# A rotation of a large matrix by 90 degrees: smaller transposing pieces and one more output buffer

## The chip, the cores and the metric

The kernel runs on one core of a Trainium2 chip. The metric is the device time of that core in microseconds (us); the median of the kernel before is 1267.99 us over 3 runs (1267.86 to 1268.66). The profile's own span of a run is about 2 us shorter than its time. No run of this study was recorded in the slow state, so all comparisons are between runs recorded as fast. A few single runs were nonetheless about 10 us longer than their fellows (one of the changed kernel, two of one experiment, and one 6 us longer); medians are quoted for that reason, and no reading rests on these runs.

## The reference

```python
def setup_inputs():
    return {"x": np.random.randn(8192, 8192).astype(np.float32), "k": 1}

def reference(x, k):
    return np.rot90(x, k)
```

No arithmetic is wanted: 268.44 MB are read, 268.44 MB are written, and every element changes its place.

## The kernel before

Each load brings 128 rows of 4096 columns (2 MB) on SyncE's queue. VectorE copies the load in chunks of `CH` columns with the columns of each block of 128 reversed, which empties the load buffer. TensorE transposes the blocks into PSUM (the tiles `pt` of the kernel), ScalarE copies PSUM into an output buffer of 2 MB, and ScalarE's queue stores it.

```python
R, W, CH, F, FP = 1024, 4096, 512, 4096, 2048      # RT = 8 loads per tile
...
a_pool = ctx.enter_context(tc.tile_pool(name="a_pool", bufs=2))    # loads
r_pool = ctx.enter_context(tc.tile_pool(name="r_pool", bufs=68))   # chunks
o_pool = ctx.enter_context(tc.tile_pool(name="o_pool", bufs=2))    # outputs
...
# load: for each of the rt blocks of 128 rows
nc.sync.dma_start(out=a[:], in_=x[r0 + t*P : r0 + (t+1)*P, c0 : c0 + W])
for j in range(W // CH):
    ar = r_pool.tile([P, CH // P, P], dt, tag="ar")
    nc.vector.tensor_copy(out=ar[:],
        in_=a[:, j*CH : (j+1)*CH].rearrange("r (b m) -> r b m", m=P)[:, :, ::-1])
    chunks[t, j] = ar
...
# store: for each half group (16 transposes of 128x128)
nc.tensor.transpose(ps[:, PW-1-w, t*P : (t+1)*P],
                    chunks[t, g*P // CH][:, g % (CH // P), :], ident)
nc.scalar.copy(o[:, G-PW-h : G-h, :], ps)
# when S blocks are filled
nc.scalar.dma_start(out=dst, in_=o[:, G-done : G-done+S, :])
```

There are 128 loads and, but for the last in two halves, 128 stores of 2 MB. With chunks of 512 columns VectorE makes 8 copies per load, 1024 in all.

Of the kernel before, what the change touches and what calls it, by code (L numbers as in the profile page):

```python
# [2 lines left out]

# [5 lines left out]

P = 128  # L10




R = 1024
RT = R // P
LAST = [4, 4]
W = 4096
CH = 512
F = 4096  # L20
FP = 2048


def whole_reads(nc):






    for fn in nc.m.functions:
        for block in fn.blocks:
            for n, ins in enumerate(block.instructions):
                if not isinstance(ins, mybir.InstDMACopy):
                    continue
                src = ins.ins[0]
                ap = [list(d) for d in src.ap]
                if len(ap) == 3 and ap[2][0] == 1 and ap[1][0] == ap[2][1]:
                    ap = [ap[0], [1, 1], [1, ap[1][1] * ap[2][1]]]
                    block.instructions[n] = copy.replace(  # L40
                        ins,
                        ins=[copy.replace(src, ap=ap)],
                        ant_dge_precooked=False,
                    )


def macro_tiles(N, M):

    tiles = [(r0, RT, c0) for r0 in range(0, N, R) for c0 in range(0, M, W)]
    r0, _, c0 = tiles.pop()  # L50
    for n in LAST:
        tiles.append((r0, n, c0))
        r0 += n * P
    return tiles


@with_exitstack
def kernel(
    ctx: ExitStack,
    tc: tile.TileContext,  # L60
    x: bass.AP,
    k: bass.AP,
    out: bass.AP,
):
    nc = tc.nc
    assert k == 1, f"only k=1 supported, got {k}"
    nc.at_finalize(whole_reads)

    N, M = x.shape
    dt = x.dtype  # L70

    consts = ctx.enter_context(tc.tile_pool(name="consts", bufs=1))
    ident = consts.tile([P, P], dt)
    make_identity(nc, ident)

    a_pool = ctx.enter_context(tc.tile_pool(name="a_pool", bufs=2))
    r_pool = ctx.enter_context(tc.tile_pool(name="r_pool", bufs=68))
    o_pool = ctx.enter_context(tc.tile_pool(name="o_pool", bufs=2))
    psum_pool = ctx.enter_context(
        tc.tile_pool(name="psum", bufs=2, space=bass.MemoryType.PSUM)  # L80
    )

    loads = 0

    def load(r0, rt, c0):





        nonlocal loads
        chunks = {}
        for t in range(rt):


            if loads < RT and loads % 4 >= 2:
                a = o_pool.tile([P, W], dt, tag="o")
            else:
                a = a_pool.tile([P, W], dt, tag="a")
            loads += 1  # L100
            nc.sync.dma_start(
                out=a[:], in_=x[r0 + t * P : r0 + (t + 1) * P, c0 : c0 + W]
            )
            for j in range(W // CH):
                ar = r_pool.tile([P, CH // P, P], dt, tag="ar")
                nc.vector.tensor_copy(  # L106
                    out=ar[:],
                    in_=a[:, j * CH : (j + 1) * CH].rearrange(
                        "r (b m) -> r b m", m=P
                    )[:, :, ::-1],  # L110
                )
                chunks[t, j] = ar
        return chunks

    def store(r0, rt, c0, chunks, end):





        rows = rt * P
        PW = 1
        while 2 * PW * rows <= FP:
            PW *= 2
        G = PW
        while 2 * G * rows <= F:
            G *= 2
        for i, g0 in enumerate(range(0, W // P, G)):
            if end and i % 2 == 0:
                ot = a_pool.tile([P, F], dt, tag="a")  # L130
            else:
                ot = o_pool.tile([P, F], dt, tag="o")
            o = ot[:, : G * rows].rearrange("m (g f) -> m g f", g=G)

            S = PW if end and r0 + rows == N and g0 + G == W // P else G
            for h in range(0, G, PW):
                pt = psum_pool.tile([P, FP], mybir.dt.float32, tag="ps")
                ps = pt[:, : PW * rows].rearrange("m (g f) -> m g f", g=PW)
                for w in range(PW):
                    g = g0 + h + w  # L140
                    for t in range(rt):
                        nc.tensor.transpose(  # L142
                            ps[:, PW - 1 - w, t * P : (t + 1) * P],
                            chunks[t, g * P // CH][:, g % (CH // P), :],
                            ident,
                        )
                nc.scalar.copy(o[:, G - PW - h : G - h, :], ps)  # L147

                done = h + PW
                if done % S == 0:  # L150
                    top = M - c0 - (g0 + done) * P
                    dst = out[top : top + S * P, r0 : r0 + rows].rearrange(
                        "(g m) f -> m g f", g=S
                    )
                    nc.scalar.dma_start(  # L155
                        out=dst, in_=o[:, G - done : G - done + S, :]
                    )

    tiles = macro_tiles(N, M)
    *most, before_last, last = tiles  # L160
    for m in most:
        store(*m, load(*m), False)

    c1 = load(*before_last)
    c2 = load(*last)
    store(*before_last, c1, True)
    store(*last, c2, True)


# [1 line left out]
_INS = ['x', 'k']  # L171
_OUTS = [((8192, 8192), 'float32')]

_NUMBERS = {'k': 1}


# [26 lines left out]
```

## Time and profile before

| | before |
|---|---|
| time, median of 3 | 1267.99 us |
| span of the profiled run | 1266.0 us |
| DMA, mean over the span | 425 GB/s |
| TensorE / ScalarE / VectorE busy | 55% / 37% / 28% |
| VectorE copies | 1024 of 512 columns |

The page gives each engine's busy time, then the span in 40 slices, of which the GB/s row matters most here. The prediction below shows those lines. Two kinds of lines also belong here: the DMA queues that carry no data of the kernel, and the time from issue to landing of the stores. These are from the page of the kernel before; a queue's line gives its packets, its MB and its share of the DMA engines' time.

```profile
q8 instruction: 32, 0.52, 0.2%
q14 instruction: 17, 0.14, 0.0%
...
out_dram<-ot ACTq DMA_DIRECT2D x127, 2048.0 KB, 15.9
```

The two queues of the kind "instruction" I take to bring the engines their programs. At 0.2% and 0.0% they look like nothing, and I passed over them.

### The profile page before, as it was taken

How to read it: one execution, taken by the hardware profiler on the slowest of the kernel's cores; microseconds unless marked ns; L12 is line 12 of the kernel's file. 1: busy time of each engine (PE TensorE's matmuls, PEld its weight loads, DVE VectorE, ACT ScalarE, POOL GpSimd, SP SyncE). 2: the span in 40 equal slices, each digit the busy share in tenths (PEclk: the TensorE clock that was granted, in tenths of full speed). 3: DMA queues.
4: the chain of work that ended last, by engine and by line, in shares of the span. 5: the costliest groups of instructions: out<-in, count | busy, mean ns of one | idle time of the engine just before them, and what ended most of it. 6: DMA issues, size and time to landing. Idle time of an engine off the chain costs nothing.

```text
span 1266.0 us, 10386 instructions
## 1 busy us (share of the span) xinstructions
PE 700.4 (55%) x4096; PEld 660.8 (52%) x4096; DVE 354.9 (28%) x1024; ACT 467.3 (37%) x257; POOL 0.7 (0%) x6
## 2 busy tenths in 40 slices
PE   1456455665655555555556546565464665656573
PEld 0355455554545455554555445464464654556573
DVE  4422322232222322233222322233222332223210
ACT  0333334333433334333433334333433334333364
POOL 0000000000000000000000000000000000000000
PEclk9986777777678777787777877778777667777687
DMA  9999999999999999999999999999999999999998
GB/s 398 416 431 429 429 428 429 430 427 430 427 429 429 429 429 430 428 429 428 430 428 428 429 429 427 427 429 426 430 429 427 414 428 430 426 427 428 428 393 370
DMA packets 37057, 537.55 MB, mean 425 GB/s; under 512 B 4112, under 2 KB 4112, under 8 KB 4112
## 3 DMA queue, kind: packets, MB, share of 16 engines
q10 hardware_dynamic: 18576, 268.44, 50.0%
q1 hardware_dynamic: 18432, 268.44, 49.9%
q8 instruction: 32, 0.52, 0.2%
q14 instruction: 17, 0.14, 0.0%
HBM read 268.44 MB, written 268.44 MB: 424 GB/s over the span
## 4 chain that ended last, share of the span: by engine, by line
DMA 78%; ACT 19%; issue 1%; DVE 1%; ACTq 0%; PE 0%; DVEq 0%
DMA out_dram<-ot 74%; ACT ot L147 19%; DMA a<-in_x_dram 3%; DVE ar L106 1%; ACTq L155 0%; PE pt L142 0%; ACTq L147 0%; DVEq L106 0%
## 5 line engine op out<-in xcount | busy, mean ns | idle before, releaser
L142 PE MATMUL pt<-ident,ar 128*128 128x128 f32 x4096 | 700.4, 350 | 548.3 <-ACT ot L147 465.9
L142 PEld LDWEIGHTS pt<-ident,ar 128*128 128x128 f32 x4096 | 660.8, 187 | 587.7 <-ACT ot L147 496.4
L147 ACT COPY ot<-pt 128x2048 f32<-128x2048 f32 x256 | 466.0, 1869 | 742.6 <-DMA out_dram<-ot 729.5
L106 DVE COPY ar<-a 128x512 f32<-128x512 f32 x1024 | 354.9, 420 | 865.8 <-DMA a<-in_x_dram 811.4
L147 ACT ACT_TABLE_LOAD x1 | 1.3, 1283 | 41.1 <-DVE ar L106 41.1
masks.py:199 POOL TENSOR_SCALAR_AFFINE_SELECT ident<-ident 128x128 f32<-128x128 f32 x1 | 0.3, 294 | 0.1
masks.py:197 POOL MEMSET ident<- 128x128 f32 x1 | 0.2, 205 | 0.3 <-POOLq L184 0.3
L184 POOL MEMSET const-bfloat16-1.0<- 128x1 bf16 x1 | 0.1, 102 | 0.0
L184 POOL MEMSET const-uint8-127<- 128x1 uint8 x1 | 0.1, 102 | 0.0
L184 POOL MEMSET const-float32-0.0<- 128x1 f32 x1 | 0.1, 99 | 0.2 <-issue 0.2
L184 POOL MEMSET const-float32-1.0<- 128x1 f32 x1 | 0.1, 99 | 0.0
## 6 DMA issues: line engine op xcount, KB each, us to landing
a<-in_x_dram SPq DMA_DIRECT2D x128, 2048.0 KB, 16.8
out_dram<-ot ACTq DMA_DIRECT2D x127, 2048.0 KB, 15.9
out_dram<-ot ACTq DMA_DIRECT2D x2, 1024.0 KB, 13.7
```

The source lines that it names most:

```text
L106: nc.vector.tensor_copy(out=ar[:], in_=a[:, j * CH : (j + 1) * CH].rearrange("r (b m) -> r b m", m=P)[:, :, ::-1],)
L142: nc.tensor.transpose(ps[:, PW - 1 - w, t * P : (t + 1) * P], chunks[t, g * P // CH][:, g % (CH // P), :], ident,)
L147: nc.scalar.copy(o[:, G - PW - h : G - h, :], ps)
L184: nc = _bacc.Bacc("TRN2", target_bir_lowering=False, num_devices=1)
```

## The change

The intent: a third output buffer should let ScalarE run further ahead of the stores, so that the DMA engines do not run dry when the loads end. Its 2 MB must come from somewhere, so the pool of chunks shrinks from 68 of 512 columns (8.5 loads' worth) to 127 of 256 (just under 8 loads, which is a whole tile); smaller chunks should come free sooner and make up for it. The first outputs go out in halves, to start the stores earlier.

```diff
-CH = 512
+CH = 256
-    r_pool = ... bufs=68
-    o_pool = ... bufs=2
+    r_pool = ... bufs=127
+    o_pool = ... bufs=3
-            if loads < RT and loads % 4 >= 2:
+            if loads < RT and loads % 5 >= 2:
-            if end and i % 2 == 0:
+            if end and i % 2:
                 ot = a_pool.tile([P, F], dt, tag="a")
-            S = PW if end and r0 + rows == N and g0 + G == W // P else G
+            starts = r0 == 0 and c0 == 0 and i < 2 or end and r0 + rows < N and i == 0
+            ends = r0 + rows == N and c0 + W == M and g0 + G == W // P
+            S = PW if starts or ends else G
 ...
-    c1 = load(*before_last)
-    c2 = load(*last)
-    store(*before_last, c1, True)
-    store(*last, c2, True)
+    *_, chunks = load(*before_last)
+    outputs = store(*before_last, chunks, True)
+    rows = load(*last)
+    for _ in range(last[1] - 1):
+        next(rows)
+    next(outputs)            # first end group ahead of the last load
+    chunks = next(rows)
+    for _ in outputs: ...
+    for _ in store(*last, chunks, True): ...
```

(`load` and `store` become generators that yield after each load and each group.)

More of the change, by code (lines that the diff above doesn't have):

```diff
@@ L76 @@
     a_pool = ctx.enter_context(tc.tile_pool(name="a_pool", bufs=2))
-    r_pool = ctx.enter_context(tc.tile_pool(name="r_pool", bufs=68))
-    o_pool = ctx.enter_context(tc.tile_pool(name="o_pool", bufs=2))
+    r_pool = ctx.enter_context(tc.tile_pool(name="r_pool", bufs=127))
+    o_pool = ctx.enter_context(tc.tile_pool(name="o_pool", bufs=3))
     psum_pool = ctx.enter_context(
@@ L112, in load @@
                 chunks[t, j] = ar
-        return chunks
+            yield chunks
     def store(r0, rt, c0, chunks, end):
@@ L157, in store @@
                     )
+            yield
     tiles = macro_tiles(N, M)
@@ L161 @@
     for m in most:
-        store(*m, load(*m), False)
-    c1 = load(*before_last)
-    c2 = load(*last)
-    store(*before_last, c1, True)
-    store(*last, c2, True)
+        *_, chunks = load(*m)
+        for _ in store(*m, chunks, False):
+            pass
+    *_, chunks = load(*before_last)
[5 more added lines that the diff above has]
+    chunks = next(rows)
+    for _ in outputs:
+        pass
+    for _ in store(*last, chunks, True):
+        pass
 _INS = ['x', 'k']
```

## The prediction

> **What bounds the kernel now.** I read the page first: busy shares, slices, the chain that ended last. Then the waits by pair, and last the time windows in steps of 100, 5 and 1 us, to find where the DMA engines are not full.
>
> ```profile
> span 1266.0 us, 10386 instructions
> PE 700.4 (55%) x4096; PEld 660.8 (52%) x4096; DVE 354.9 (28%) x1024; ACT 467.3 (37%) x257; POOL 0.7 (0%) x6
> ...
> GB/s 398 416 431 429 429 428 429 430 427 430 427 429 429 429 429 430 428 429 428 430 428 428 429 429 427 427 429 426 430 429 427 414 428 430 426 427 428 428 393 370
> ...
> DMA 78%; ACT 19%; issue 1%; DVE 1%; ACTq 0%; PE 0%; DVEq 0%
> L106 DVE COPY ar<-a 128x512 f32<-128x512 f32 x1024 | 354.9, 420 | 865.8 <-DMA a<-in_x_dram 811.4
> ```
>
> No engine is busy more than 55% of the span, while the GB/s row stays at 426 to 431 in 35 of the 40 slices. The chain is DMA for 78%; the 19% of ACT in it is copying while other transfers run, so it is no cost by itself. The waits say the same from the other side:
>
> ```profile
> DVE ar L106 <- DMA a<-in_x_dram: 811.4, 121, 8.1
> ACT ot L147 <- DMA out_dram<-ot: 729.5, 118, 6.9
> ```
>
> VectorE waits for a load 121 times and ScalarE for an output buffer 118 times, out of 128 of each: both sides stand behind the same transfers. A queue that waits for its buffer costs nothing as long as the other queue, or an earlier transfer of its own, fills the engines. So the question is only where both run dry.
>
> ```profile
> 0.00:5.00 5.00, 0.00 (x0) 0.00 (x0) 0.00 (x0) 0.00 (x0) 0.70 (x6) 1.00 0.65 226
> ...
> 100.00:1100.00 1000.00, 563.81 (x3252) 534.21 (x3253) 280.11 (x809) 371.24 (x204) 0.00 (x0) 0.74 1.01 428
> ...
> 1214.00:1215.00 1.00, 1.00 (x6) 1.00 (x6) 0.00 (x0) 1.00 (x1) 0.00 (x0) 0.50 0.43 180
> 1215.00:1216.00 1.00, 1.00 (x7) 1.00 (x6) 0.00 (x0) 0.43 (x1) 0.00 (x0) 0.50 0.16 66
> 1216.00:1217.00 1.00, 1.00 (x8) 1.00 (x7) 0.00 (x0) 0.00 (x0) 0.00 (x0) 0.66 0.69 295
> ```
>
> The last two columns are the DMA share and GB/s. In the middle 1000 us the share is 1.01 and the rate 428. The hole stands at 1214 to 1217.
>
> The account: 537.55 MB in all, at the 429 GB/s of the best long stretches, take 537.55 / 0.429 = 1253.0 us. The span has 13.0 more. By windows of 5 us, each charged with (429 minus its rate) / 429 of its length: the first 5 us lose 2.4 (no byte can move before the first load starts); 45 to 65, when stores join the loads, lose 0.9 (426, 416, 374, 423); 1210 to 1225 lose 2.3 (378, 334, 374); 1225 to 1260, where only stores are left, lose 0.9 (410 to 423); the last 6 us hold only 193 GB/s over 5 us and lose 3.75 (the last bytes land and are confirmed). That is 10.3; the other 2.7 are the difference of 426 to 428 from 429 over the long middle.
>
> Why there is a hole at 1214, from the timeline:
>
> ```profile
> 1205.62 0.55 ACTq L155 DMA_DIRECT2D out_dram<-ot  x1
> 1208.10 2.77 DVE L106 COPY ar<-a 128x512 f32<-128x512 f32 x8 [7.04 <-DMA a<-in_x_dram]
> 1211.80 3.63 ACT L147 COPY ot<-pt 128x2048 f32<-128x2048 f32 x2 [6.21 <-DMA out_dram<-ot]
> ...
> 1215.46 0.55 ACTq L155 DMA_DIRECT2D out_dram<-ot  x1
> 1217.14 3.65 ACT L147 COPY ot<-pt 128x2048 f32<-128x2048 f32 x2 [1.71 <-PE pt L142]
> ```
>
> With two output buffers one store is in flight while the other buffer waits for its landing (1211.72), is filled for 3.63 us, and is issued at 1215.46. While loads share the engines a store takes 9.8 us of them and that turnaround is hidden. The last load is issued at 1201.1; when its bytes run out, the one store left finishes in half the time and nothing is queued behind it. Then at 1217.14 ScalarE waits 1.71 us for TensorE, which could not begin that group before ScalarE freed PSUM at 1213.7.
>
> [...] here a load takes 4.9 us alone (copies start at 8.10, 12.99, 17.88) and 9.8 us beside stores. [...]
>
> **The change part by part.**
> 1. *Chunks of 256.* 2048 VectorE copies for 1024. [...] Sixteen per load are 3.4 us for 2.77: +0.6 per load, 80 us of busy time in all, 28% to about 34%. None of it is on the path: VectorE sits 7.0 us idle before each load in the steady stretch. A load buffer comes back 0.6 us later, with another load already queued.
> 2. *127 chunks of 256 for 68 of 512.* A tile of 8 loads uses 128 of the small ones. The spare goes from 4 large (half a load) to minus 1 small, but chunks come free after each half group rather than each group. In the built programs VectorE's copies take the chunks in the order in which TensorE frees them, so one group of stores makes room for one load in both.
> 3. *Third output buffer.* ScalarE, and TensorE behind it, run one group further ahead of the stores. That frees one load's worth of chunks earlier, more than the half load lost in part 2. Steady rate unchanged: the DMA share is already 1.01. At the end two stores (about 10 us of engine time at 4.9 to 5.0 each) instead of one stand queued when the last load's bytes run out, against a turnaround of about 4 us (3.63 + 0.1 of issue and a start): the hole at 1210 to 1225 should close. I count 2.0 of its 2.3 us.
> 4. *First outputs in halves.* The first store goes after one copy, about 1.9 us sooner than 49.65. But loads fill the engines at 419 to 433 GB/s until 50, so it only reorders. Of the 0.9 lost at 45 to 65 I count 0.3. Three more issues at 0.55 us of ScalarE's queue are beside 6 us waits. The first group of the next-to-last piece in halves helps the same hole as part 3, not a second one.
> 5. *Five load buffers at the start for four.* Loads alone already run at about 430 GB/s with four; nothing.
> 6. *The last load's chunks allocated after the first end group.* Needed because 8 loads of chunks no longer fit; TensorE has that group early, so no wait follows.
>
> Sum: -2.0 - 0.3 = -2.3 us; 1268.0 - 2.3 = 1265.7.
>
> **Rivals.**
> *Chunks become the wait.* With no spare, VectorE waits for TensorE, a load buffer stays full, loads pause. For it: VectorE already waited 54.4 us on TensorE, 7 times, up to 12.0. Against: during those waits (55.8 to 67.8) stores kept the share at about 1, and three output buffers give TensorE more lead. If it emptied the load queue for 1 us in each of the 15 later tiles, the time would be about 1280.
> *It was hidden anyway.* The hole merely moves later, for instance to ScalarE's pace at the end (4.31 us per group against about 5.0 of DMA). Then 1268 stays. Against: ScalarE is the faster of the two, and its last copy ends 11 us before the DMA engines go quiet.
> *A larger gain.* All of 2.3 and 0.9, and 428 becoming 429 through the deeper store queue (1100 us x 1/429 = 2.6): 1262. Against: a share of 1.01 leaves nothing for a deeper queue to fill.
>
> **Range and chances.** Fixed losses (2.4 first, 3.75 last, 0.9 for stores alone) and the 1253.0 put the floor near 1260 of span, 1262 of time (the time is 2.0 above the span). Gain between 0 and 5 us, so 1262.8 to 1268.2 for 8 in 10. Two per cent is 25 us, twice all the time that is not at full rate: faster by that is nearly excluded; slower by that would need a new wait in every tile.
>
> **What would show it.** Right: the GB/s row unchanged in the middle; its last two slices up from 393 and 370; no window under 300 GB/s between 1205 and 1250; VectorE near 435 us busy and its copies near 212 ns apart; ScalarE's waits for stores still the largest of its waits. Wrong: VectorE waiting for TensorE well above 54 us together with steady windows under 425; a hole left at the end of the loads; or a first slice different from 398 by more than 10.

## The result, and the profile after

| | before | after |
|---|---|---|
| median of 6 runs | 1267.97 us | 1274.97 us |
| lowest to highest | 1267.50 to 1268.66 | 1274.66 to 1284.05 |
| ratio of fast runs | | 1.0066, 95% interval 1.0039 to 1.0093 |

The kernel became 7.0 us slower by the medians. That is within 2%, as I had expected, but outside my range and in the other direction. A ratio here is the mean time of one kernel's fast runs over that of the other's of the same rounds, so it isn't quite the ratio of the medians; the one run of 1284 us lifts it.

The page of the changed kernel answers to the lines of the prediction:

```profile
span 1272.9 us, 11534 instructions
PE 702.6 (55%) x4096; PEld 662.8 (52%) x4096; DVE 425.6 (33%) x2048; ACT 466.8 (37%) x257; POOL 0.7 (0%) x6
...
GB/s 397 423 427 428 428 428 429 428 429 429 428 429 427 429 429 430 428 429 428 429 430 428 426 424 427 427 427 423 429 424 427 425 423 423 428 426 419 424 374 328
...
q14 instruction: 26, 0.21, 0.0%
...
DMA 82%; ACT 13%; DVE 2%; PE 2%; ACTq 0%; issue 0%; SPq 0%; DVEq 0%
L106 DVE COPY ar<-a 128x256 f32<-128x256 f32 x2048 | 425.6, 287 | 796.7 <-DMA a<-in_x_dram 578.2
...
out_dram<-ot ACTq DMA_DIRECT2D x124, 2048.0 KB, 25.6
```

The bound is still DMA, with 82% of the chain. VectorE's busy time is 425.6 us. The rate starts as before, but sinks in the second half: of the slices from the 22nd on many read 423 to 426, where before had mostly 426 to 430. The last two are 374 and 328, against 393 and 370, where I had expected a rise. A store lands 25.6 us after its issue instead of 15.9, which only says that more stores are under way: with one issued every 9.8 us (median, both kernels) 2.6 on average for 1.6, an estimate from these three numbers.

The waits of the changed kernel, by pair (total us, times, longest):

```profile
ACT ot L149 <- DMA out_dram<-ot: 698.9, 113, 8.8
DVE ar L106 <- DMA a<-in_x_dram: 578.2, 94, 8.0
...
DVE ar L106 <- PE pt L144: 218.6, 34, 7.8
```

The page now puts 34 of VectorE's waits, 218.6 us, down to TensorE, that is to a free chunk (54.4 us and 7 times before). That is the line that I had named as the sign of my first rival. It is a temptation: the line has grown by 164 us, the time by 7, and it need not be the cause. In the trace the copy that ends each of the 34 waits also starts 0.09 to 0.12 us after the 16th landing of a load, so each of them was a wait for a load as well.

The windows of the changed kernel at the end of the loads and at the very end (stretch, us, busy time of five engines, granted clock, DMA share, GB/s):

```profile
1100.00:1200.00 100.00, 57.23 (x326) 54.43 (x325) 33.78 (x163) 36.35 (x20) 0.00 (x0) 0.74 1.01 424
...
1216.00:1217.00 1.00, 1.00 (x5) 1.00 (x6) 0.00 (x0) 1.00 (x1) 0.00 (x0) 0.50 0.54 229
1217.00:1218.00 1.00, 1.00 (x7) 1.00 (x6) 0.00 (x0) 0.70 (x1) 0.00 (x0) 0.50 0.27 115
1218.00:1219.00 1.00, 1.00 (x6) 1.00 (x5) 0.01 (x1) 0.00 (x0) 0.00 (x0) 0.50 0.43 180
...
1260.00:1265.00 5.00, 0.00 (x0) 0.00 (x0) 0.00 (x0) 0.00 (x0) 0.00 (x0) 0.50 0.98 408
1265.00:1270.00 5.00, 0.00 (x0) 0.00 (x0) 0.00 (x0) 0.00 (x0) 0.00 (x0) 0.50 0.22 90
...
1269.00:1270.00 1.00, 0.00 (x0) 0.00 (x0) 0.00 (x0) 0.00 (x0) 0.00 (x0) 0.50 0.06 25
```

Two things are to be seen. There is still a hole at 1216 to 1219, though another store now stands in the queue. And the end has a tail of more than 5 us in which the DMA share is 0.22, or as much as 3 to 4 engines of 16. Before, the stretch 1260 to 1265 held 193 GB/s and the next microsecond none. From 1268 to 1271 the share is 0.06 in each microsecond, which is one engine of 16. So most DMA engines finish, and a few, in the end one, do not. The GB/s row, a mean of 16 engines, can't show that.

### One level below the page: 16 landings per transfer

The trace has 16 landing events for each of the 257 transfers of before and the 260 of after, as many as the page has DMA engines; I take each to be one engine's. The next instruction starts after the 16th: in the changed kernel VectorE's first copy after each of the 128 loads starts 0.02 to 0.12 us after the 16th landing, when the first is 5.9 us past (median). So I read the time of this kernel, bound by DMA, as that of its slowest DMA engine.

I therefore took from the trace's records of landings, for each transfer in order, the time of its 16th landing, counted from the start of the span, less 4.877 us for each 2 MB landed so far (two 1 MB halves count as one). 4.877 us is the steady time of 2 MB where nothing disturbs (4.873 to 4.883 from the first to the last landing on each of the treads below that begin at 715 or later), so what remains is the time that the slowest DMA engine has lost. (These records are in the packed trace; no view of the page shows them, and they don't name the DMA engine. That it is the same one over a stretch is inferred from how its losses add up. Where the loads end the number falls by about two us (24.0 to 21.6 and 22.4 in the changed kernel), I suppose because fewer transfers are under way at once; so compare like stages.) The changed kernel between 694 and 1214 us, one number per change:

```
time of landing  lost by the slowest engine (us, from 16.3 at 694)
694 to 704       0.00
715 to 773       0.95
779 to 833       1.90
843 to 902       2.86
908 to 961       3.81
972 to 1031      4.75 to 4.86
1036 to 1090     5.78
1101 to 1155     6.74
1160 to 1214     7.68
```

It is a staircase. On a tread, 12 or 13 transfers in a row, the loss moves by a few hundredths of a microsecond, in one place by a tenth; then it jumps by about 0.95 us within one or two transfers. Set beside the 8 KB packets of the queue q14 the jumps have an owner. Eight of them start at 708, 777, 837, 906, 966, 1035, 1095 and 1155 us: one at each jump, and no jump without one. (Three others, at 797, 980 and 1114 us, leave no mark on the slowest DMA engine.) They take 309 ns. In the records a 16 KB read packet of the loads begins 0.31 us after each, as the fetch ends, and takes 1211 to 1216 ns in place of the usual 611. Together that is 0.31 + 0.60 = 0.91 us of one DMA engine. Before 694 us the changed kernel's picture is less clean: from about 260 to 655 us the slowest DMA engine is mostly another, which slips by some 0.11 us per load without such fetches, and the one with the steps follows close behind. The cleanest case is e1 below: from 150 to 1200 us its slowest DMA engine loses 15.4 us, and 16 such fetches lie there, 0.96 us each.

I take these packets for VectorE's instructions, because their number follows VectorE's: the trace has 1358 instruction records of VectorE before and 2505 after, 1147 more, and the page has 26 packets on q14 for 17, 9 more. That is one packet of 8 KB for about 127 instructions (an estimate from these two differences). VectorE doesn't stand still for it: the starts of its copies of one load are at most 0.211 us apart in the whole trace of after (median 0.202). But one DMA engine does.

| | before | after |
|---|---|---|
| 8 KB fetches followed by a read of over 1.2 us, whole span | 11 | 18 |
| of these from 150 to 1200 us | 9 | 16 |
| distance between them | about 118 us | 60 to 69 us |
| loss of the slowest DMA engine at 150 us | 8.5 | 9.3 |
| at 700 us | 12.4 | 16.3 |
| at 1200 us | 17.3 | 24.0 |
| at the last landing | 16.5 | 23.3 |

(Each loss but the last is a mean over the last four transfers before that time.) At 1200 us the difference is 6.7 and at the last landing 6.8, of the 6.9 by which the spans differ. From 150 to 1200 us the slowest engine loses 14.7 us after and 8.8 before, so 5.9 of the 6.7 arise there, evenly. Seven fetches more at 0.95 would make 6.7. It is less because before, from about 294 us on, the slowest DMA engine is another one, which slips by about 0.08 us at each load without any fetch and has besides two steps of 0.8 us, at fetches of q14 at 346 and 975 us that are not in VectorE's rhythm; the engine with VectorE's fetches ended 1.4 us ahead of it.

### The profile page after: what moved, and what is told of

Its sections match the earlier page's. It is cut to its first block, busy times and chain, and to the rows that moved or that the text cites. A ratio compares the mean times of both kernels' runs of the same rounds, so it can differ in the third digit from the quotient of the medians.

```text
span 1272.9 us, 11534 instructions
## 1 busy us (share of the span) xinstructions
PE 702.6 (55%) x4096; PEld 662.8 (52%) x4096; DVE 425.6 (33%) x2048; ACT 466.8 (37%) x257; POOL 0.7 (0%) x6
## 4 chain that ended last, share of the span: by engine, by line
DMA 82%; ACT 13%; DVE 2%; PE 2%; ACTq 0%; issue 0%; SPq 0%; DVEq 0%
DMA out_dram<-ot 71%; ACT ot L149 13%; DMA a<-in_x_dram 11%; DVE ar L106 2%; PE pt L144 2%; ACTq L157 0%; ACTq L149 0%; SPq L101 0%; DVEq L106 0%
## 5 line engine op out<-in xcount | busy, mean ns | idle before, releaser
L106 DVE COPY ar<-a 128x256 f32<-128x256 f32 x2048 | 425.6, 287 | 796.7 <-DMA a<-in_x_dram 578.2
## 6 DMA issues: line engine op xcount, KB each, us to landing
out_dram<-ot ACTq DMA_DIRECT2D x124, 2048.0 KB, 25.6
```

The source lines that it names most:

```text
L106: nc.vector.tensor_copy(out=ar[:], in_=a[:, j * CH : (j + 1) * CH].rearrange("r (b m) -> r b m", m=P)[:, :, ::-1],)
```

## The experiments

The theory after this reading is **fetch**: twice as many VectorE instructions mean twice as many fetches, each of which holds up the same one DMA engine for 0.95 us. The rivals are **depth** (the third output buffer lets the DMA engines drift apart and costs time), **chunks** (the pool with no spare makes VectorE wait for TensorE, and loads are late) and, later, **turnaround** (16 small copies return a load buffer 0.6 us later). Every run below gave a correct result and was timed against the kernel before in 5 rounds. Ratios are to before in the same rounds; the medians of before were 1267.99 in the first four runs, 1267.84 in the next four and 1268.62 in the last four (three groups on three chips).

| run | what it is | median us | ratio (95%) | loss of the slowest engine at 150 / 700 / 1200 us |
|---|---|---|---|---|
| e1 | before, chunks of 256, 136 of them | 1274.76 | 1.0052 (1.0040 to 1.0064) | 8.5 / 16.2 / 23.9 |
| e2 | after, chunks of 512 | 1267.32 | 1.0001 (0.9987 to 1.0015) | 8.7 / 12.6 / 16.4 |
| e3 | after, two output buffers | 1277.67 | 1.0098 (1.0071 to 1.0126) | 8.8 / 16.9 / 24.7 |
| e7 | after, half the chunks on GpSimd | 1270.85 | 1.0023 (1.0010 to 1.0035) | 9.6 / 13.7 / 19.4 |
| e8 | before, chunks of 1024 | 1266.85 | 0.9990 (0.9977 to 1.0002) | 8.2 / 11.3 / 15.6 |
| e9 | before, each chunk by two copies | 1273.99 | 1.0045 (1.0033 to 1.0058) | 8.2 / 16.2 / 23.0 |
| e10 | before, chunks of 128 | 1314.81 | 1.0371 (1.0357 to 1.0385) | 10.1 / 35.1 / 58.1 |
| e12 | after, first outputs whole | 1275.65 | 1.0058 (1.0046 to 1.0071) | 8.4 / 17.1 / 24.9 |

Not in this table are e4, e5 and e6, which became something else than what I meant, and e11, in which another wait took over.

### e1: the small chunks alone

```diff
-CH = 512
+CH = 256
-    r_pool ... bufs=68
+    r_pool ... bufs=136
```

> Kernel before with chunks of 256 alone (136 of them, the same memory as 68 of 512; two output buffers). Three theories for the 7.0 us lost. Fetch theory (1024 more VectorE instructions are fetched by the same DMA engines, ten more 8 KB fetches, and one DMA engine that already lags carries them): slower than before by 3 to 7 us, last landing spread over the 16 engines near 6 us instead of 2.8. Depth theory (the third output buffer lets the 16 DMA engines drift apart, 18 us between first and last of one store instead of 8 to 9, and the end pays for it): as before, within 1 us. Chunk theory (no spare chunk, VectorE waits for TensorE): as before, since there are spares here.

1274.76 us. Two output buffers, a full pool, whole first outputs, the old order at the end, and the loss is all there, in the time and in the staircase (23.9 at 1200 us). So depth, and a pool with no spare, are not needed for it. Two things did not come as expected. The spread of the last landing is 2.1 us and not near 6. And by the page VectorE waits longer for TensorE even with spare chunks; the runs e8 and e3 show why that wait is no measure of the loss:

```profile
DVE ar L106 <- PE pt L142: 190.5, 28, 11.5
DVE ar L106 <- PE pt L142: 82.8, 14, 7.4
DVE ar L106 <- PE pt L144: 83.5, 112, 2.0
```

The lines are those of e1, e8 and e3, in this order. e8 and e3 have the same 83 us of it in total, and their medians are 10.8 us apart (1266.85 and 1277.67).

### e2: everything but the small chunks

```diff
 # the changed kernel with
-CH = 256
+CH = 512
-    r_pool ... bufs=127
+    r_pool ... bufs=63
```

> Changed kernel with chunks of 512 again (63 of them, as 127 of 256 one or two short of a tile), everything else as changed: three output buffers, halves, end order. Fetch theory: back near 1268 or below, since the instruction count is that of before. Depth theory: stays near 1275, spread of one store still 15 to 18 us. Chunk theory: at or above 1275, since room comes back in whole groups only and VectorE waits longer for TensorE (above 219 us in all).

1267.32 us, where before stands at 1267.99: the loss is gone with the small chunks. The first and last landing of a transfer lie up to 13.8 us apart in this run, 9.5 in before and 18.7 in the changed kernel, so a third buffer does let the DMA engines drift further apart; but that in itself costs nothing here. This run is also the fair test of my prediction's idea, the third buffer by itself. The medians give it 0.7 us of the 2.3 that I had promised, and the ratio 1.0001 gives it none.

### e3: the third buffer taken back

```diff
 # the changed kernel with
-    o_pool ... bufs=3
+    o_pool ... bufs=2
-            if loads < RT and loads % 5 >= 2:
+            if loads < RT and loads % 4 >= 2:
```

> Changed kernel with two output buffers again (and four load buffers at the start), 127 chunks of 256 kept. Fetch theory: stays at 1271 to 1275. Depth theory: back to 1267 to 1269, spread of one store at most 9 us. Chunk theory: slower than the changed kernel, above 1276, as TensorE loses its lead and VectorE waits longer for chunks.

1277.67 us, slower than the changed kernel by 2.7 in the medians, so depth as a cost is refuted: the third buffer helps here. The fetch theory alone had given 1271 to 1275, so the size is missed. The chunk theory's number, above 1276, is met, but not its wait: by the page VectorE waits 83.5 us for TensorE, less than the 218.6 of the changed kernel. This kernel has 127 chunks where e1, also with two buffers, had 136 and took 2.9 us less, and the end is arranged differently. The landings put more than half of the 2.9 at the end: between 1232 and 1247 us, where only stores are left, e3's slowest DMA engine goes from 23.1 to about 25.0 and e1's from 22.3 to 22.6. What in the end's order does it, and the rest, stay open.

### e4, e5, e6: three tries that tested something else

To test the count of instructions or the turnaround by themselves I added idle work on VectorE to the kernel before: one `memset` of one column per chunk (e4), a copy of one column out of the load buffer per chunk (e5), and one copy of 1024 columns more per load (e6).

```diff
+    scrap = consts.tile([P, 1], dt)            # e6: [P, 1024]
 ...
 # one of these:
+                nc.vector.memset(scrap[:], 0.0)                                      # e4, per chunk
+                nc.vector.tensor_copy(out=scrap[:], in_=a[:, j*CH : j*CH + 1])       # e5, per chunk
+            nc.vector.tensor_copy(out=scrap[:], in_=a[:, :1024])                     # e6, per load
```

> Kernel before with 1024 one-column memsets on VectorE, which add instructions and no data. Fetch theory: slower than before by 3 to 7 us, with about 8 more 8 KB instruction fetches, as e1. Depth and chunk theories: as before within 1 us.

> Kernel before with a one-column VectorE copy after each of its 1024 copies (it reads the load buffer, so it cannot be moved away as the memsets were). The traces of before and changed show the slowest of the 16 DMA engines jump by about 0.95 us at each 8 KB fetch of VectorE's instructions, every 118 us before and every 60 us after. Fetch theory: the instruction count is that of the changed kernel, so the fetches come every 60 us, that engine loses 10 x 0.95 more, and the time is 1272 to 1277. Turnaround theory (VectorE gives a load buffer back 0.6 us later): the tiny copies also lengthen it by some 0.6 us, so 1272 to 1277 too; the next run tells the two apart. Third possibility, that the copies of 256 columns themselves matter: 1268.

> Kernel before with one VectorE copy of 1024 columns more for each load: about 0.61 us [...] later release of each load buffer, as in the changed kernel (3.33 for 2.77 us), with only 128 more instructions, one more fetch. Fetch theory: within 1.5 us of before. Turnaround theory: slower by about 7 us, as e1.

(The text of e5 puts the jumps of before on its slowest DMA engine; from 294 us on they are on the second slowest. e6's 0.61 us was an estimate of mine; in its trace such a copy is 0.61 us from its start, at 629.57, to the next one's, at 630.18.)

They took 1291.65, 1594.76 and 1524.90 us, and none of it says anything on fetches. The added instructions didn't stay where I had written them. In e4, the timeline (start, us, group) shows them drawn forward:

```profile
115.74 5.59 DVE L113 MEMSET scrap<- 128x1 f32 x45
```

45 of them run in a row in the first part of the kernel, where the rate falls to 287 GB/s in a slice; once they are used up (the last starts at 260.8 us), the rate is 419 to 430 in each slice until the last two. In e6 the added copy of the *next* load stands amid the copies of this one:

```profile
629.57 0.69 DVE L114 COPY scrap<-a 128x1024 f32<-128x1024 f32 x1 [14.38 <-DMA a<-in_x_dram]
```

VectorE waits 14.4 us for a load there, and the first of the eight copies behind it in its queue starts only at 630.18. By my reading four of them are of the load before, whose buffer can't be returned until then. The loads then go one at a time: SyncE waits for VectorE before 116 of them, 1238.9 us in all. In e5 it is the same, before 115 loads and for 1443.9 us. So these are kernels with a new wait, and the lesson is to look at the order of instructions, and not just at the source, before a run is spent.

### e7: the same chunks, half of VectorE's instructions

```diff
 # the changed kernel with
-                nc.vector.tensor_copy(
+                by = nc.gpsimd if j % 2 else nc.vector
+                by.tensor_copy(
```

> Changed kernel with every second chunk copied by GpSimd, so that neither engine's instruction stream has more than VectorE's had before. Fetch theory: no single DMA engine carries all the fetches, so faster than the changed kernel by 4 to 7 us (1268 to 1271), if GpSimd's fetches go through another DMA engine; as the changed kernel (1275) if they go through the same one. Turnaround theory: GpSimd's copies are slower, so the buffers come back later still, and it is slower than 1275.

1270.85 us, 4.1 less than the changed kernel. This tells fetch from turnaround, because the turnaround stays the same: from the timeline, VectorE and GpSimd work side by side and are done 3.36 us after the first copy began, against 3.33 in the changed kernel. GpSimd's copies are a little slower, as the turnaround theory had it (eight in 3.34 us for 3.11 of VectorE's eight), but a load buffer comes back only 0.03 us later.

```profile
606.17 3.11 DVE L107 COPY ar<-a 128x256 f32<-128x256 f32 x8 [6.74 <-DMA a<-in_x_dram]
606.19 3.34 POOL L107 COPY ar<-a 128x256 f32<-128x256 f32 x8 [6.51 <-DMA a<-in_x_dram]
```

The number of instructions and of q14 fetches is no lower than in the changed kernel:

```profile
q14 instruction: 28, 0.23, 0.0%
```

But the fetches in VectorE's rhythm now come about every 109 us, 11 with a read of over 1.2 us in the span for 18, and the others do not add to them on the slowest DMA engine. So it isn't the sum of fetches that counts but how many one DMA engine gets. The loss at 1200 us is 19.4, and 2.1 above before; what is left is the slipping engine, at 0.10 us per load in place of 0.08.

### e8 and e10: larger and smaller chunks in the kernel before

```diff
-CH = 512
+CH = 1024      # e8, r_pool bufs=34
+CH = 128       # e10, r_pool bufs=272
```

> Kernel before with chunks of 1024 (34 of them): half of its VectorE instructions, fetches every 200 us or more. Fetch theory: that DMA engine gains 5 x 0.95, but another DMA engine, 1.4 us behind it already in the trace of before, stays, so 0 to 1.5 us faster than before at most. Turnaround theory: 0.3 us less per load, faster by up to 3 us. If room for chunks in larger pieces matters, slower.

> Kernel before with 272 chunks of 128: 4096 VectorE copies. Fetch theory, as a dose: about 20 fetches more than e1, 20 x 0.95 = 19 us more on the DMA engine that carries them, so 1288 to 1298. If the number of instructions matters otherwise (a threshold, a phase between the DMA engines): no such proportion, 1270 to 1280.

e8 took 1266.85 us. Its page:

```profile
span 1264.3 us, 9798 instructions
...
q14 instruction: 12, 0.10, 0.0%
```

There are 12 fetches for 17, of VectorE's 5 with a read of over 1.2 us for 11. The gain is about 1 us by the medians, as expected small, because in before the slowest DMA engine is already the one that slips, not the one with the fetches. The interval of its ratio ends at 1.0002, so that it is faster isn't shown. It has the lowest median of the study all the same.

e10 took 1314.81 us. The direction is right, but it overshoots the 1288 to 1298 that I had written down. VectorE has 4096 copies and a fetch about every 40 us, and the steps are there, from 0.95 to 1.6 us each; but from 150 to 1200 us the slowest DMA engine loses 48.0 us, and the 26 fetches of that stretch at 0.95 are 24.7, about half. Between these steps, some 20 us after a fetch, the slowest engine has others of 0.5 to 1.0 us; in the stretch that I looked at closely (500 to 700 us) no packet of q8 or q14 starts at them, but just before them the reads of many DMA engines are long at once. The records have 471 data packets of over 1.1 us between 100 and 1200 us, for 37 in before. VectorE's wait for TensorE, as the page has it, also grows:

```profile
DVE ar L106 <- PE pt L142: 345.2, 62, 10.6
```

I can't tell cause from consequence there, and the surplus of e10 stays open.

### e9: twice the copies, the chunks as before

```diff
-                nc.vector.tensor_copy(out=ar[:], in_=a[:, j*CH : (j+1)*CH]...)
+                for h in (0, 2):
+                    nc.vector.tensor_copy(out=ar[:, h:h+2, :],
+                        in_=a[:, j*CH + h*P : j*CH + h*P + 256]...)
```

> Kernel before, its 68 chunks of 512 kept, but each written by two VectorE copies of 256 columns, one after the other: the instruction count of the changed kernel with the room, buffers and stores of before. Fetch theory: 1273 to 1277, VectorE's fetches every 60 us and the slowest DMA engine jumping 0.95 us at each. If the finer pool of chunks were the cause in e1: 1268.

This is what e4 to e6 should have been: 2048 VectorE copies, but 68 chunks of 512 columns and two output buffers. It took 1273.99 us, 5.4 above before. Its page:

```profile
q14 instruction: 25, 0.20, 0.0%
...
L107 DVE COPY ar<-a 128x256 f32<-128x256 f32 x2048 | 425.4, 287 | 800.8 <-DMA a<-in_x_dram 686.7
```

Of the 25 fetches 18 are followed by a read of over 1.2 us, and the steps at them are 0.95 to 0.99. So the size and the number of the chunks in the pool do not cost the time, but the copies do. By this run alone it could be their number or the later return of the load buffer; e7 keeps the second and gains. Together with e7 this is the strongest pair of the study: e9 adds instructions and leaves the buffers alone, e7 leaves the buffers alone and takes the instructions away from VectorE.

### e11: a pool with no spare in large pieces

```diff
 # the changed kernel with
-CH = 256
+CH = 1024
-    r_pool ... bufs=127
+    r_pool ... bufs=31
```

> Changed kernel with 31 chunks of 1024: fewest instructions, third output buffer and halves kept. Fetch theory: as e8 or slightly better, 1265.5 to 1267, unless room that comes back only after two groups makes VectorE wait for TensorE and the loads stop; then slower than before.

1326.37 us (ratio 1.0454, 1.0440 to 1.0469). VectorE has few instructions, and the kernel is slow for quite another reason, which the GB/s row and one of the waits of this run show:

```profile
GB/s 402 423 425 429 427 430 386 427 366 427 428 361 430 368 422 430 365 428 370 423 428 359 430 382 415 429 359 431 383 409 428 362 429 384 407 429 361 432 426 379
```

```profile
ACT ot L149 <- PE pt L144: 384.2, 57, 25.0
```

Every second or third slice, about once in each tile of 8 loads, the rate falls to some 360 GB/s. The pool is one short of a whole tile, and the missing piece is now a quarter of a load. The page puts 16 of VectorE's waits, once per tile, 97.9 us, down to TensorE. This is what my first rival described, and this is how it looks: dips in the mean rate. The changed kernel has no such dips, though the page puts more of its VectorE's waits down to TensorE (218.6 us in total). So the rival exists, but at 256 columns no run needs it.

### e12: the first outputs whole

```diff
 # the changed kernel with
-            S = PW if starts or ends else G
+            S = PW if ends else G
```

> Changed kernel with the first outputs stored whole again (the last one still in halves). All theories: within 0.7 us of the changed kernel, 1274.3 to 1275.7, since the DMA engines are full when those stores start.

(The edit also makes the first group of the next-to-last piece whole.) 1275.65 us and a ratio of 1.0058, against 1274.97 and 1.0066 for the changed kernel. The halves change nothing that these runs can tell.

## Why the prediction was wrong

**What bounds the kernel** was right in kind: DMA, before and after (78% and 82% of the chain). It was wrong in the measure. I took the mean rate of the 16 DMA engines as the clock of the kernel, and a share of 1.01 as proof that nothing was left to lose. The time of these runs follows the slowest DMA engine, which accounts for 6.8 of the 6.9 us by which the spans differ. To "the difference of 426 to 428 from 429 over the long middle" I gave 2.7 us and no cause; the slowest DMA engine of that same kernel lost 8.8 us between 150 and 1200 us. And the 3.75 us of the last 6 that I took as fixed are in part its tail: the DMA share is 0.26 and 0.18 at 1262 to 1264, four and three DMA engines of 16.

**Part 1, chunks of 256**, holds the step that failed: "None of it is on the path". What I worked out there came true. VectorE is busy for 425.6 us (I had said near 435), its copies follow each other in 3.33 / 16 = 0.208 us (I had said 0.212; both were estimates of mine, like the 3.4 us per load, made before any run had copies of 256 columns), and its waiting before the loads hides them. But I priced the instructions only on the engine that runs them. In these traces an 8 KB packet also goes with about each 127 of them (9 packets, 1147 instructions), over the DMA engines that are the bound: a read of 1.21 us for 0.61 follows 18 of the 26 in the changed kernel. The term missing from the sum was 7 to 9 more fetches of 0.95 us on one DMA engine. e1 and e9 show it alone (+6.8 and +5.4 us by the medians), e2 shows the kernel without it.

**Part 2, 127 chunks**: I had feared the missing spare and judged it harmless. VectorE's wait for TensorE, as the page has it, went up to 218.6 us, and yet the change is explained without it; e1 has the same loss with 136 chunks, and e8 and e3 have the same wait without the same time. In larger pieces the fear would have been right (e11). What 127 in place of 136 cost with two buffers (e3, part of 2.9 us) stays unclear.

**Part 3, the third buffer**: "I count 2.0 of its 2.3 us" failed as well. The hole is still there at 1216 to 1219, and in before it wasn't worth what I charged. There the store on its way across the hole has its 16th landing at 1219.81, and the next one, issued in the hole at 1215.46, at 1224.86: 5.05 us later, where the 2 MB stores after it follow at 4.72 to 5.34. So the slowest engine lost next to nothing in the hole; those that idled were the DMA engines ahead of it. In the changed kernel they are further ahead: the last store issued before the hole lands first at 1216.07 and for the 16th time at 1227.03. A hole in the mean isn't a hole in the slowest. e2 gives the whole part 0.7 us at most.

**Part 4, halves**: 0.3 us counted; e12 shows no difference. (The 5 us windows up to 50 us read 419 to 442, and not to 433 as I wrote; it changes nothing.) The first store did go at 47.79 us and not 49.65, as predicted, and it was worth as little as said. **Part 5**, the fifth load buffer: the first slice reads 397 for 398, nothing, as said. **Part 6**: no run separates it.

**The rivals.** "It was hidden anyway" is the fate of the gain. "Chunks become the wait" named the right direction, with the wrong mechanism, and its sign (a longer wait of VectorE for TensorE together with steady windows under 425) came true, with 424 in the stretch 1100 to 1200. A sign that another cause can also give doesn't tell the two apart; e1 did. "A larger gain" was out of reach for the same reason as part 3. None of the three was the fetch.

**What stays open.** The DMA engine that slips by about 0.07 us per load in e8, 0.08 in before, 0.10 in e7 and 0.11 in the changed kernel, without fetches of VectorE on it: I know its pace, not its cause. Nor is it shown why the read after a fetch takes 0.60 us longer; the records give the order and the times only. And there is the end of e3, and e10's surplus.

## What to carry to other kernels

In a kernel bound by DMA, count instructions even on an engine that is mostly idle: here each additional 127 or so of VectorE's cost one DMA engine 0.95 us, so copies of 512 columns were better than twice as many of 256 (1267.99 and 1274.76 us, e1) beyond what they do to the engine itself. There is little to gain once another DMA engine is the slowest (e8: 1 us, not clear of noise), and larger pieces can bring a wait of their own (e11). Take the landings one DMA engine at a time before believing that a steady rate (428 GB/s here), or a hole in it, says where the time goes. And when a wait that you feared does show up after a change, still undo it alone before you blame it.
